# Low parts of weights from GpSimd to VectorE, and sums of squares by TensorE, in the first stage of a two-layer encoder trunk

## The chip, the cores and the metric

The kernel runs on one core of one Trainium2 chip. The metric is the device time of one execution in microseconds (us), taken as the median of several runs. A second, profiled execution leaves a trace of what each engine did: TensorE (PE, with its weight loads apart as PEld), VectorE (DVE), ScalarE (ACT), GpSimd (POOL) and SyncE (SP, which here issues every DMA).

## The reference

Two layers over x of 512 rows and 2048 columns, float32. Each layer is conditioned by a vector c of 2048: a product with a 2048 x 6144 matrix gives a shift, a scale and a gate.

```python
shift, scale, gate = split(silu(c) @ w_mod + b_mod, 3)
h = rms_norm(x, norm_g) * (1.0 + scale) + shift
out = mixer(h)                # projection in, attention and convolution, or spatial gating; projection out
x = x + gate * out
```

`rms_norm` divides a row by the root of the mean of its squares. After the two layers there is one more `rms_norm`.

## The kernel before

Everything lies transposed: a page is 128 of the 2048 features by the 512 rows. x has 16 pages (`x_t[0]` to `x_t[15]`), and so has h. Products on TensorE are made in three passes, to keep float32 precision: each operand is split into a high part (a rounded copy, fp32r) and a low part (the rest), and `mm3` (lines 371 to 376) adds high x high, high x low and low x high.

The change lies in the first stage, up to about 262 us, in which h is made and already used:

- **The norm.** ScalarE squares the 16 pages of x (L656). VectorE adds the 16 squares up into one page (L660, L661). Four small products with ones sum that page over the features (L207), VectorE scales and adds EPS (L210), GpSimd takes the power -1/2 (L211), VectorE multiplies the identity by it (L218), one product spreads it over all partitions (L224), ScalarE copies it to `R` (L225).
- **The conditioning.** `mod_tile(n, nt)` (L250 to L258) loads 128 columns of the conditioning matrix as two tiles of 128x1024 (`mraw`, five buffers) and multiplies each by silu(c), with the sum kept (L255). A page of h needs two such pairs, four products: the scale's pair, after which L262 makes the factor `gsc`, and the shift's pair, which gives `mod`.
- **A page of h**, `modulated(kt)`: VectorE x * gsc * R into `tmp` (L610), ScalarE the high part (L614, the page `hh`), VectorE the low part (L617, the page `lh`).
- **Weights.** `split_w` loads a tile `wraw` (three buffers), ScalarE casts it to the high part `whi` (L674), and **GpSimd** subtracts for the low part `wlo` (L675). There are 16 tiles of 128x768 (`in_ab_wp`, one per page) and 48 of 128x512 (`in_ab_wg`).
- **TensorE.** Per page, `mm3` for six gates: 18 matmuls of 512 columns, which need `hh`, `lh`, `whi` and `wlo`. For every four pages and each of three groups g, `quarter(g, q)` multiplies four pages with four tiles into two alternating PSUM banks: 48 matmuls, with a sum into SBUF after each 12 (ScalarE copies the first quarter, L699; VectorE adds the later ones, L701). Together 16 x 18 + 12 x 48 = 864 matmuls. The last of them, `quarter(2, 3)`, ends the stage; the projections and the attention follow on TensorE without a gap.

A scheduler fixes, when the program is built, the order in which each engine runs its instructions. At run time an engine takes them strictly in that order and waits at the first that isn't ready; SP's DMA issues are one such queue too.

```python
for kt in range(KT):
    with tc.issue_after(total.ins):
        mod_tile(pa, "ab", KT + kt, 5)
    mod_scale("ab", kt)
    mod_tile(pa, "ab", kt, 5)
    hi, lo = split_w(ab_wp[kt], W_P, work, 2)
    modulated("ab", kt, x_t[kt], r0, h.add())
```

`issue_after(total.ins)` puts the first products behind the last addition of squares (L661).

Of the kernel before, what the change touches and what calls it, by code (L numbers as in the profile page):

```python
# [9 lines left out]
F32 = mybir.dt.float32  # L10
F32R = mybir.dt.float32r
AF = mybir.ActivationFunctionType
ALU = mybir.AluOpType

D = 2048
S = 512
P = 128
KT = D // P
NT = S // P
HEADS = 8  # L20
GROUPS = 8
EPS = 1e-6
# [4 lines left out]
ALL, LEFT, RIGHT = slice(0, S), slice(0, S // 2), slice(S // 2, S)  # L27
# [88 lines left out]
def trunk(ctx, tc, xT, vecs, ab_wm, sg_wm, ab_wp, ab_wg, ab_wi, ab_wo, sg_wi, sg_wo, wsT, bs, rope, band, eye, out):  # L116
    nc = tc.nc
# [9 lines left out]
    def page(tag, bufs, dt=F32, pool=None):  # L127
        return (pool or work).tile([P, S], dt, tag=tag, bufs=bufs, name=tag)
# [44 lines left out]
    def bank():  # L173
        return psum.tile([P, S], F32, tag="ps", name="ps")
# [6 lines left out]
    ones = const.tile([P, P], F32, name="ones")  # L181
# [9 lines left out]
    x_t = Pages()  # L191
# [5 lines left out]
    def v1(c):  # L197
        return vec[:, c:c + 1]


    def inverse(parts, cols=ALL):
        n = (cols.stop - cols.start) // P
        sums = [bank() for _ in range(n)]
        for j, s in enumerate(parts):
            for i, acc in enumerate(sums):
                ts = slice(cols.start + i * P, cols.start + (i + 1) * P)
                nc.tensor.matmul(acc[:, 0:1], lhsT=s[:, ts], rhs=ones[:, 0:1], start=j == 0, stop=j == len(parts) - 1)  # L207
        r4 = const.tile([P, NT], F32, tag="r4", bufs=2, name="r4")
        for i, acc in enumerate(sums):
            nc.vector.tensor_scalar(out=r4[:, i:i + 1], in0=acc[:, 0:1], scalar1=1.0 / D, scalar2=EPS, op0=ALU.mult, op1=ALU.add)  # L210
        nc.gpsimd.tensor_tensor(out=r4[:, :n], in0=r4[:, :n], in1=mhalf[:, :n], op=ALU.pow)  # L211
        return r4

    def rms(parts, cols=ALL):
        r4, n = inverse(parts, cols), (cols.stop - cols.start) // P
        dg = page("tmp", 4)
        for i in range(n):
            nc.vector.tensor_scalar(out=dg[:, i * P:(i + 1) * P], in0=ident, scalar1=r4[:, i:i + 1], scalar2=None, op0=ALU.mult)  # L218
        return dg

    def spread(dg, r, cols=ALL):
        n = cols.stop - cols.start
        pr = bank()
        nc.tensor.matmul(pr[:, :n], lhsT=ones, rhs=dg[:, :n], start=True, stop=True)  # L224
        nc.scalar.copy(out=r[:, cols], in_=pr[:, :n])  # L225
# [24 lines left out]
    def mod_tile(pool, n, nt, bufs):  # L250
        src, b = wm[n]
        for h in range(2):
            raw = pool.tile([P, HALF], F32, tag="mraw", bufs=bufs, name="mraw")
            nc.sync.dma_start(out=raw, in_=src[nt, h])
            nc.vector.tensor_tensor_reduce(  # L255
                out=raw, in0=raw, in1=cb[:, h * HALF:(h + 1) * HALF], scale=0.5,
                scalar=v1(b + nt) if h == 0 else macc[n][:, nt:nt + 1], op0=ALU.mult, op1=ALU.add,
                accum_out=(mods if h else macc)[n][:, nt:nt + 1])  # L258

    def mod_scale(n, kt):  # L260
        g = v1((V_ABG if n == "ab" else V_SGG) + kt)
        nc.vector.scalar_tensor_tensor(  # L262
            out=gsc[n][:, kt:kt + 1], in0=mods[n][:, KT + kt:KT + kt + 1], scalar=1.0, in1=g,
            op0=ALU.add, op1=ALU.mult)
# [106 lines left out]
    def mm3(acc, w, m, first, last, **kw):  # L371


        nc.tensor.matmul(acc, lhsT=w[0], rhs=m[0], start=first, stop=False, **kw)  # L374
        nc.tensor.matmul(acc, lhsT=w[0], rhs=m[1], start=False, stop=False, **kw)  # L375
        nc.tensor.matmul(acc, lhsT=w[1], rhs=m[0], start=False, stop=last, **kw)  # L376

    class Pos:
# [3 lines left out]
        def slice(self):  # L382
            w = self.s.next(self.i, self.more)
            self.i += 1
            if self.tick:
                self.tick(self.s.last.ins)
            return w
# [216 lines left out]
                    mm3(acc, (a[0][:, ts], a[1][:, ts]), (hi[:, cs], lo[:, cs]), kt == 0, kt == KT - 1)  # L604
        return accs

    def modulated(n, kt, t, r, to, cols=ALL, keep=False):

        xr = page("tmp", 4)
        nc.vector.scalar_tensor_tensor(  # L610
            out=xr[:, cols], in0=t[:, cols], scalar=gsc[n][:, kt:kt + 1], in1=r[:, cols], op0=ALU.mult, op1=ALU.mult)
        hi, lo = to
        sh = mods[n][:, kt:kt + 1]
        nc.scalar.activation(out=hi[:, cols], in_=xr[:, cols], func=AF.Identity, bias=sh)  # L614
        if keep:
            nc.scalar.activation(out=t[:, cols], in_=xr[:, cols], func=AF.Identity, bias=sh)
        nc.vector.scalar_tensor_tensor(  # L617
            out=lo[:, cols], in0=xr[:, cols], scalar=sh, in1=hi[:, cols].bitcast(F32), op0=ALU.add, op1=ALU.subtract)

    def twice_silu(acc, s):  # L620

# [27 lines left out]
    h = Parts()  # L649
    pos = Pos(s_abi, s_abo)  # L650
    pa = tc.alloc_tile_pool(name="pa", bufs=2, reuse_waits="tile")
    parts = []
    squares = Book("hh", F32)
    for kt in range(KT):
        sq = squares.page()
        nc.scalar.activation(out=sq, in_=x_t[kt], func=AF.Square)  # L656
        if kt < 2:
            parts.append(sq)
        else:
            nc.vector.tensor_tensor(out=parts[kt % 2], in0=parts[kt % 2], in1=sq, op=ALU.add)  # L660
    total = nc.vector.tensor_tensor(out=parts[0], in0=parts[0], in1=parts[1], op=ALU.add)  # L661
    r0 = page("R", 2)
    spread(rms(parts[:1]), r0)

    def split_w(src, n, pool, bufs):
        raw = work.tile([P, HALF], F32, tag="wraw", bufs=3, name="wraw")[:, :n]
        size = HALF if pool is work else n  # L670
        hi = pool.tile([P, size], F32R, tag="whi", bufs=bufs, name="whi")[:, :n]
        lo = pool.tile([P, size], F32R, tag="wlo", bufs=bufs, name="wlo")[:, :n]
        nc.sync.dma_start(out=raw, in_=src)
        nc.scalar.copy(out=hi, in_=raw)  # L674
        nc.gpsimd.tensor_tensor(out=lo, in0=raw, in1=hi.bitcast(F32), op=ALU.subtract)  # L675
        return hi, lo

    gates = [bank() for _ in range(6)]
    sums, held = {}, {}

    def fetch(g, kts):
        for kt in kts:
            held[g, kt] = split_w(ab_wg[g, kt], S, pa, 8)

    def quarter(g, q):
        if q == 0:
            sums[g] = pa.tile([P, 4, S], F32, tag="sum", bufs=1, name="sum") if g == 1 else work.tile([P, 4, S], F32, tag="xy", bufs=4, name="xy")
        for f in range(4):
            acc = bank()
            cs = slice(f * P, (f + 1) * P)  # L690
            for i in range(4):
                kt = 4 * q + i
                (hi, lo), a = held[g, kt], h[kt]
                if g:
                    mm3(acc, (hi[:, cs], lo[:, cs]), a, i == 0, i == 3)
                else:
                    mm3(acc, (a[0][:, cs], a[1][:, cs]), (hi, lo), i == 0, i == 3)
            if q == 0:
                nc.scalar.copy(out=sums[g][:, f], in_=acc)  # L699
            else:  # L700
                nc.vector.tensor_tensor(out=sums[g][:, f], in0=acc, in1=sums[g][:, f], op=ALU.add)  # L701

    for kt in range(KT):
        with tc.issue_after(total.ins):
            mod_tile(pa, "ab", KT + kt, 5)
        mod_scale("ab", kt)
        mod_tile(pa, "ab", kt, 5)
        hi, lo = split_w(ab_wp[kt], W_P, work, 2)
        modulated("ab", kt, x_t[kt], r0, h.add())
        for f in range(6):  # L710
            cs = slice(f * P, (f + 1) * P)
            mm3(gates[f], (hi[:, cs], lo[:, cs]), h[kt], kt == 0, kt == KT - 1)
        fetch(0, [kt])
        q, i = divmod(kt, 4)
        if q:
            at = 4 * (q - 1) + 2 * (i % 2)
            fetch(1 + i // 2, [at, at + 1])
            if i % 2:
                quarter(1 + i // 2, q - 1)
        if i == 3:  # L720
            quarter(0, q)
# [188 lines left out]
    h = Parts()  # L910
# [22 lines left out]
    parts = right()  # L933
# [6 lines left out]
    for part in (0, 2):  # L940
        for kt in range(KT):
            hi, lo = ws[kt // 2]
# [56 lines left out]
    for n in range(4):  # L999
# [3 lines left out]
        for j in range(NT):  # L1003
            t = y.g[n][:, j]
# [3 lines left out]
    for i in range(2):  # L1008
        acc = bank()
# [61 lines left out]
    for g in range(2):  # L1071
        for i in range(2):
            turned_block(g, i)
    parts = right()
    r4 = inverse(parts, RIGHT)
    for f in (KT - 2, KT - 1):
        nc.scalar.activation(out=x3[f][:, RIGHT], in_=x3[f][:, RIGHT], func=AF.Copy, scale=v1(V_FG + f))
# [4 lines left out]
    for i in range(2):  # L1082
        for g in range(4):
            t = fin[i][:, g]
# [4 lines left out]
            if g % 2:  # L1089
                (nc.scalar if g > 1 else nc.sync).dma_start(  # L1090
                    out=out[1].rearrange("(t p n) -> t p n", t=2, p=P)[i, :, (g - 1) * S:(g + 1) * S].rearrange("p (g s) -> p g s", g=2),
                    in_=fin[i][:, g - 1:g + 1])
    left = out[0].rearrange("(f p n) -> f p n", f=KT, p=P)
    for f in range(KT):
        t = x3[f][:, LEFT]
# [81 lines left out]
```

## Time and profile before

| what | value |
|---|---|
| median of 3 runs | 1674.51 us (1673.35 to 1674.95) |
| profiled execution, its own time | 1674.59 us |
| span of its trace, first to last instruction | 1672.5 us |
| PE busy | 1616.3 us, 97% |
| DVE busy | 1307.8 us, 78% |
| ACT busy | 664.5 us, 40% |
| POOL busy | 146.0 us, 9% |

The profiled execution's own time is 2.1 us above its span. Busy shares are means over the whole span; the change is in the first sixth, and there the shares are others. A busy PE is not a PE at its peak, since the ends of matmuls are modelled: what counts is how many matmuls of 512 columns it starts in a stretch.

### The profile page before, as it was taken

To read this page: it belongs to the slowest core of one execution; us is meant where nothing else is said; L and a number is where in the kernel's file an instruction comes from. 1 tells how busy PE (TensorE), PEld (TensorE's weight loads), DVE (VectorE), ACT (ScalarE), POOL (GpSimd) and SP (SyncE) were. 2 spreads that over 40 slices of the span, in tenths; PEclk is the share of its full clock that TensorE was granted. 3 is DMA by queue.
4 is the path that set the end of the run, shared out by engine and by line. 5 is a ranking of instruction groups with operands and counts; after the bars stand their busy time and mean duration, and the time that the engine had idled before them with its cause. 6 is when DMAs were issued, how large, how long until landed. Compare 5 with 4: busy or idle time off the path is not lost.

```text
span 1672.5 us, 24676 instructions
## 1 busy us (share of the span) xinstructions
PE 1616.3 (97%) x9900; PEld 1442.9 (86%) x9900; DVE 1307.8 (78%) x1761; ACT 664.5 (40%) x953; POOL 146.0 (9%) x95
## 2 busy tenths in 40 slices
PE   4799899999999999999999999999999999999998
PEld 3677787888888888888889998999999999998998
DVE  7899738867765867677778878787988788898884
ACT  3232234323322323233544545444444444465552
POOL 2466531000000000000000000000000000000000
PEclk7999999999999999999999999999999999999999
DMA  8777534665666666655364351333233323335333
GB/s 314 255 266 271 199 111 160 223 219 196 218 214 232 233 211 215 213 199 195 102 217 138 124 170 57 107 110 102 87 114 95 118 94 119 96 100 200 105 98 115
DMA packets 85538, 276.44 MB, mean 165 GB/s; under 512 B 8752, under 2 KB 11056, under 8 KB 85424
## 3 DMA queue, kind: packets, MB, share of 16 engines
q1 hardware_dynamic: 85136, 273.82, 48.7%
q8 instruction: 77, 1.26, 0.3%
q10 hardware_dynamic: 288, 1.05, 0.2%
q14 instruction: 37, 0.30, 0.1%
HBM read 266.45 MB, written 8.39 MB: 164 GB/s over the span
## 4 chain that ended last, share of the span: by engine, by line
PE 82%; DVE 11%; issue 3%; ACT 2%; DMA 1%; SPq 0%; POOL 0%; POOLq 0%; DVEq 0%; ACTq 0%
PE ps L376 27%; PE ps L374 27%; PE ps L375 27%; DVE mraw L255 4%; DVE wlo L310 1%; PE ps L1028 1%; PE ps L783 1%; DVE gsc_ab L262 1%; ACT whi L309 1%; DMA xy<-in_xT_dram 1%; DVE lh L617 0%; ACT hh L614 0%; DVE st L1007 0%; DVE third L310 0%; DVE wraw L318 0%
## 5 line engine op out<-in xcount | busy, mean ns | idle before, releaser
L374 PE MATMUL ps<-hh,whi 128*128 128x512 f32 (+1 forms) x1600 | 570.1, 359 | 21.7 <-ACT hh L614 16.3
L375 PE MATMUL ps<-lh,whi 128*128 128x512 f32 (+1 forms) x1600 | 569.0, 356 | 1.5 <-DVE lh L845 1.5
L376 PE MATMUL ps<-hh,wlo 128*128 128x512 f32 (+1 forms) x1600 | 568.9, 356 | 1.2 <-DVE wlo L310 1.2
L374 PEld LDWEIGHTS ps<-hh,whi 128*128 128x128 f32 x1600 | 305.4, 191 | 68.9 <-ACT hh L614 20.0
L309 ACT CAST whi<-wraw 128x1024 fp32r<-128x1024 f32 x190 | 199.8, 1052 | 399.4 <-PE ps L375 289.9
L375 PEld LDWEIGHTS ps<-lh,whi 128*128 128x128 f32 x1600 | 305.0, 191 | 44.0 <-DVE lh L845 1.9
L376 PEld LDWEIGHTS ps<-hh,wlo 128*128 128x128 f32 x1600 | 304.9, 191 | 44.1 <-DVE wlo L310 1.7
L310 DVE TENSOR_TENSOR wlo<-wraw,whi 128x1024 fp32r<-128x1024 f32 x190 | 232.5, 1225 | 107.1 <-ACT whi L309 106.5
L255 DVE CUSTOM_DVE_ANT_0 mraw<-mraw,cb,vec 128x1024 f32<-128x1024 f32 x96 | 138.2, 1440 | 21.4 <-DMA mraw<-in_sg_wm_dram 16.7
L675 POOL TENSOR_TENSOR wlo<-wraw,whi 128x512 fp32r<-128x512 f32 (+1 forms) x64 | 117.2, 1851 | 104.6 <-ACT whi L674 97.9
L376 PE MATMUL ps<-sum,wlo 128*128 128x256 f32 x408 | 113.0, 277 | 0.9 <-DVE wlo L310 0.9
L374 PE MATMUL ps<-sum,whi 128*128 128x256 f32 x408 | 112.7, 276 | 0.0
L375 PE MATMUL ps<-sum,whi 128*128 128x256 f32 x408 | 112.7, 276 | 0.0
L374 PE MATMUL ps<-whi,hh 128*128 128x512 f32 (+1 forms) x288 | 102.8, 357 | 2.1 <-DVE xy L701 2.0
L309 ACT CAST whi<-first 128x1024 fp32r<-128x1024 f32 x56 | 58.8, 1050 | 114.0 <-DVE first L318 65.9
L375 PE MATMUL ps<-wlo,hh 128*128 128x512 f32 (+1 forms) x288 | 102.1, 354 | 0.3 <-POOL wlo L675 0.3
L376 PE MATMUL ps<-whi,lh 128*128 128x512 f32 (+1 forms) x288 | 102.1, 355 | 0.0
L310 DVE TENSOR_TENSOR wlo<-first,whi 128x1024 fp32r<-128x1024 f32 x56 | 68.3, 1220 | 24.8 <-ACT whi L309 24.8
L255 DVE CUSTOM_DVE_ANT_0 mraw<-mraw,cb,macc_ab 128x1024 f32<-128x1024 f32 x48 | 76.3, 1591 | 3.1 <-DMA mraw<-in_ab_wm_dram 2.1
L376 PEld LDWEIGHTS ps<-sum,wlo 128*128 128x128 f32 x408 | 76.6, 188 | 1.4 <-DVE wlo L310 1.4
L318 DVE TENSOR_TENSOR first<-first,wraw 128x1024 f32<-128x1024 f32 x63 | 76.7, 1217 | 0.5
L375 PEld LDWEIGHTS ps<-sum,whi 128*128 128x128 f32 x408 | 76.6, 188 | 0.0
(255 smaller groups left out, 2861.4 us busy)
## 6 DMA issues: line engine op xcount, KB each, us to landing
mraw<-in_ab_wm_dram SPq DMA_DIRECT2D x96, 512.0 KB, 4.6
mraw<-in_sg_wm_dram SPq DMA_DIRECT2D x96, 512.0 KB, 4.5
wraw<-in_ab_wi_dram SPq DMA_DIRECT2D x92, 512.0 KB, 3.7
wraw<-in_sg_wi_dram SPq DMA_DIRECT2D x75, 512.0 KB, 3.5
wraw<-in_ab_wo_dram SPq DMA_DIRECT2D x27, 512.0 KB, 3.5
wraw<-in_sg_wo_dram SPq DMA_DIRECT2D x27, 512.0 KB, 3.5
wraw<-in_ab_wg_dram SPq DMA_DIRECT2D x48, 256.0 KB, 2.9
first<-in_sg_wi_dram SPq DMA_DIRECT2D x21, 512.0 KB, 3.5
```

What stands on the lines that cost most here:

```text
L255: nc.vector.tensor_tensor_reduce(out=raw, in0=raw, in1=cb[:, h * HALF:(h + 1) * HALF], scale=0.5, scalar=v1(b + nt) if h == 0 else macc[n] ...
L262: nc.vector.scalar_tensor_tensor(out=gsc[n][:, kt:kt + 1], in0=mods[n][:, KT + kt:KT + kt + 1], scalar=1.0, in1=g, op0=ALU.add, op1=ALU.mult)
L309: nc.scalar.copy(out=hi, in_=raw)
L310: nc.vector.tensor_tensor(out=lo, in0=raw, in1=hi.bitcast(F32), op=ALU.subtract)
L318: nc.vector.tensor_tensor(out=r[a], in0=r[a], in1=r[b], op=ALU.add)
L374: nc.tensor.matmul(acc, lhsT=w[0], rhs=m[0], start=first, stop=False, **kw)
L375: nc.tensor.matmul(acc, lhsT=w[0], rhs=m[1], start=False, stop=False, **kw)
L376: nc.tensor.matmul(acc, lhsT=w[1], rhs=m[0], start=False, stop=last, **kw)
L675: nc.gpsimd.tensor_tensor(out=lo, in0=raw, in1=hi.bitcast(F32), op=ALU.subtract)
L783: nc.tensor.transpose(out=pt[:, i * P:(i + 1) * P], in_=ps[i][:, ks], identity=ident)
L1028: nc.tensor.matmul(accs[f][:, j * P:(j + 1) * P], lhsT=y.g[n][:, j, f * P:(f + 1) * P], rhs=wst[g // 4][:, g % 4 * P:(g % 4 + 1) * P], sta ...
```

## The change

Three edits, all in the first stage.

1. `split_w`: the subtraction that makes `wlo` is issued on VectorE, no longer on GpSimd.
2. The squares: no additions on VectorE. Each page of squares is the moving operand (512 columns) of a product whose weights are a single column of ones, so that the sums stand in one row of 512 in PSUM. ScalarE copies that row, four small products turn it into a column of four, and the rest of the norm is as before, with one instruction for L210 where there were four.
3. `modulated` takes `meanwhile`: the next page's scale pair (two products and `gsc`) is emitted inside it, and the low part of a page is placed behind the first of these two products. The first page's pair stands ahead of the loop, with no `issue_after`.

```diff
-        r4, n = inverse(parts, cols), (cols.stop - cols.start) // P
+        return diagonal(inverse(parts, cols), (cols.stop - cols.start) // P)
...
+        with ExitStack() as after:
+            if meanwhile:
+                after.enter_context(tc.issue_after(meanwhile()))
+            nc.vector.scalar_tensor_tensor(
+                out=lo[:, cols], in0=xr[:, cols], scalar=sh, in1=hi[:, cols].bitcast(F32), op0=ALU.add, op1=ALU.subtract)
...
+    row = bank()
     for kt in range(KT):
         sq = squares.page()
         nc.scalar.activation(out=sq, in_=x_t[kt], func=AF.Square)
-        if kt < 2:
-            parts.append(sq)
-        else:
-            nc.vector.tensor_tensor(out=parts[kt % 2], in0=parts[kt % 2], in1=sq, op=ALU.add)
-    total = nc.vector.tensor_tensor(out=parts[0], in0=parts[0], in1=parts[1], op=ALU.add)
+        nc.tensor.matmul(row[0:1], lhsT=ones[:, 0:1], rhs=sq, start=kt == 0, stop=kt == KT - 1)
+    line = page("tmp", 4)
+    nc.scalar.copy(out=line[0:1], in_=row[0:1])
+    turned = bank()
+    for i in range(NT):
+        nc.tensor.matmul(turned[:, i:i + 1], lhsT=line[0:1, i * P:(i + 1) * P], rhs=ones[0:1, 0:1], start=True, stop=True)
     r0 = page("R", 2)
-    spread(rms(parts[:1]), r0)
+    spread(diagonal(root([turned[:, :NT]], NT), NT), r0)
...
-        nc.gpsimd.tensor_tensor(out=lo, in0=raw, in1=hi.bitcast(F32), op=ALU.subtract)
+        nc.vector.tensor_tensor(out=lo, in0=raw, in1=hi.bitcast(F32), op=ALU.subtract)
...
+    def scale(kt):
+        began = mod_tile(pa, "ab", KT + kt, 5)
+        mod_scale("ab", kt)
+        return began
+
+    scale(0)
     for kt in range(KT):
-        with tc.issue_after(total.ins):
-            mod_tile(pa, "ab", KT + kt, 5)
-        mod_scale("ab", kt)
         mod_tile(pa, "ab", kt, 5)
         hi, lo = split_w(ab_wp[kt], W_P, work, 2)
-        modulated("ab", kt, x_t[kt], r0, h.add())
+        modulated("ab", kt, x_t[kt], r0, h.add(), meanwhile=(lambda: scale(kt + 1)) if kt < KT - 1 else None)
```

The lines move by 7 to 19 in the changed file: L255 is L262 there, L262 is L272, L610 is L621, L617 is L631, L675 is L691, L701 is L717.

The order that VectorE gets, between the copies of `cb` (silu(c) spread out) and the first page's L610. Each product is an `ISA` row on `mraw`, with a second row that reads its sum. Before:

```order
L661 TENSOR_TENSOR hh<-hh 128x512
L255 ISA mraw,macc_ab<-mraw,cb,vec 128x1024
L255 ISA macc_ab 128x1
L210 TENSOR_SCALAR r_172<-ps 128x1 x4
L255 ISA mraw,mod_ab<-mraw,cb,macc_ab 128x1024
L255 ISA mod_ab 128x1
L218 TENSOR_SCALAR tmp<-ident,r_172 128x128 x4
```

And from the same place of the changed program:

```order
L262 ISA mraw,mod_ab<-mraw,cb,macc_ab 128x1024
L262 ISA mod_ab 128x1
L691 TENSOR_TENSOR wlo<-wraw,whi 128x768
L215 TENSOR_SCALAR r_173<-ps 128x4
L262 ISA mraw,macc_ab<-mraw,cb,vec 128x1024
L262 ISA macc_ab 128x1
L225 TENSOR_SCALAR tmp<-ident,r_173 128x128 x4
L262 ISA mraw,mod_ab<-mraw,cb,macc_ab 128x1024
L262 ISA mod_ab 128x1
L691 TENSOR_TENSOR wlo<-wraw,whi 128x512
```

Four products stand ahead of L215 now (the last of them is the first row shown) and two more, with two low parts of weights, ahead of the first L621; before, four products stood ahead of the first L610.

VectorE again, one page further on in the loop, between the `tmp` of two pages. Before:

```order
L610 SCALAR_TENSOR_TENSOR tmp<-xy,gsc_ab,R 128x512
L255 ISA mraw,macc_ab<-mraw,cb,vec 128x1024
L255 ISA macc_ab 128x1
L255 ISA mraw,mod_ab<-mraw,cb,macc_ab 128x1024
L255 ISA mod_ab 128x1
L617 SCALAR_TENSOR_TENSOR lh<-tmp,mod_ab,hh 128x512
L255 ISA mraw,macc_ab<-mraw,cb,vec 128x1024
L255 ISA macc_ab 128x1
L255 ISA mraw,mod_ab<-mraw,cb,macc_ab 128x1024
L255 ISA mod_ab 128x1
L262 SCALAR_TENSOR_TENSOR gsc_ab<-mod_ab,vec 128x1
```

Now, from the `tmp` of page 4 to that of page 5:

```order
L621 SCALAR_TENSOR_TENSOR tmp<-xy,gsc_ab,R 128x512
L262 ISA mraw,macc_ab<-mraw,cb,vec 128x1024
L262 ISA macc_ab 128x1
L262 ISA mraw,mod_ab<-mraw,cb,macc_ab 128x1024
L262 ISA mod_ab 128x1
L691 TENSOR_TENSOR wlo<-wraw,whi 128x768
L262 ISA mraw,macc_ab<-mraw,cb,vec 128x1024
L262 ISA macc_ab 128x1
L631 SCALAR_TENSOR_TENSOR lh<-tmp,mod_ab,hh 128x512
L262 ISA mraw,mod_ab<-mraw,cb,macc_ab 128x1024
L262 ISA mod_ab 128x1
L691 TENSOR_TENSOR wlo<-wraw,whi 128x512
```

The low part of the page (L617, now L631) has moved behind one more product, and the low parts of the weights stand between the products.

TensorE at the start of the program. Before:

```order
L241 MATMUL ps<-ident,cs 128x128 x16
L207 MATMUL ps<-ones,hh 128x1 x4
L224 MATMUL ps<-tmp,ones 128x512
L374 MATMUL ps<-hh,whi 128x512 x6
```

And now:

```order
L248 MATMUL ps<-ident,cs 128x128 x16
L672 MATMUL ps<-hh,ones 1x512 x16
L677 MATMUL ps<-ones,tmp 128x1 x4
L231 MATMUL ps<-tmp,ones 128x512
L384 MATMUL ps<-hh,whi 128x512 x6
```

Sixteen products over 512 columns stand ahead of the small ones; nothing else in TensorE's first rows has moved.

## Rows read from the trace of the kernel before

**Rows 1.** The page, busy us, share of the span and instructions by engine.
```profile
PE 1616.3 (97%) x9900; PEld 1442.9 (86%) x9900; DVE 1307.8 (78%) x1761; ACT 664.5 (40%) x953; POOL 146.0 (9%) x95
```

**Rows 2.** Stretches: us, busy us of PE, PEld, DVE, ACT, POOL (instructions), clock, DMA.
```profile
12.00:14.00 2.00, 0.00 (x0) 0.00 (x0) 2.00 (x5) 1.87 (x5) 0.00 (x0) 0.98 1.07 417
14.00:16.00 2.00, 0.00 (x0) 0.00 (x0) 2.00 (x4) 1.50 (x3) 0.00 (x0) 0.50 1.03 421
...
100.00:120.00 20.00, 17.26 (x69) 13.74 (x69) 17.92 (x19) 8.36 (x14) 12.42 (x7) 0.91 0.79 271
```

**Rows 3.** Who waited for whom, 26 to 262 us: total us, times, longest.
```profile
POOL wlo L675 <- ACT whi L674: 97.9, 29, 13.0
...
PE ps L374 <- ACT hh L614: 16.3, 6, 3.0
...
PE ps L374 <- DVE xy L701: 4.8, 3, 2.8
...
PE ps L374 <- DVE sum L701: 2.0, 1, 2.0
```

**Rows 4.** VectorE by form, 20 to 262 us: busy us, mean ns, idle before.
```profile
L255 DVE CUSTOM_DVE_ANT_0 mraw<-mraw,cb,macc_ab 128x1024 f32<-128x1024 f32 x32 | 55.9, 1747 | 0.8
L255 DVE CUSTOM_DVE_ANT_0 mraw<-mraw,cb,vec 128x1024 f32<-128x1024 f32 x31 | 51.5, 1661 | 1.4 <-DMA mraw<-in_ab_wm_dram 1.4
L617 DVE SCALAR_TENSOR_TENSOR lh<-tmp,mod_ab,hh 128x512 fp32r<-128x512 f32 x16 | 19.2, 1201 | 10.4 <-ACT hh L614 10.4
...
L610 DVE SCALAR_TENSOR_TENSOR tmp<-xy,gsc_ab,R 128x512 f32<-128x512 f32 x16 | 15.0, 937 | 0.8 <-ACT R L225 0.2
L262 DVE SCALAR_TENSOR_TENSOR gsc_ab<-mod_ab,vec 128x1 f32<-128x1 f32 x16 | 14.8, 922 | 0.4
```

**Rows 5.** Timeline, VectorE then GpSimd, around 60 us: start us, us, instruction.
```profile
52.72 1.67 DVE L262 SCALAR_TENSOR_TENSOR gsc_ab<-mod_ab,vec 128x1 f32<-128x1 f32 x1
54.52 0.75 DVE L610 SCALAR_TENSOR_TENSOR tmp<-xy,gsc_ab,R 128x512 f32<-128x512 f32 x1
55.19 1.28 DVE L255 CUSTOM_DVE_ANT_0 mraw<-mraw,cb,vec 128x1024 f32<-128x1024 f32 x1
...
56.51 1.28 DVE L255 CUSTOM_DVE_ANT_0 mraw<-mraw,cb,macc_ab 128x1024 f32<-128x1024 f32 x1
...
62.92 0.16 DVE L262 SCALAR_TENSOR_TENSOR gsc_ab<-mod_ab,vec 128x1 f32<-128x1 f32 x1
...
51.78 2.60 POOL L675 TENSOR_TENSOR wlo<-wraw,whi 128x768 fp32r<-128x768 f32 x1 [1.51 <-ACT whi L674]
```

**Rows 6.** Timeline, the high part of page 3 and the stage's last two sums.
```profile
57.83 0.72 ACT L614 ACTIVATE hh<-tmp,mod_ab 128x512 fp32r<-128x512 f32 x1 [6.13 <-DVE mod_ab L255]
...
258.82 0.69 DVE L701 TENSOR_TENSOR xy<-ps,xy 128x512 f32<-128x512 f32 x1 [2.03 <-PE ps L376]
261.54 0.69 DVE L701 TENSOR_TENSOR xy<-ps,xy 128x512 f32<-128x512 f32 x1 [2.03 <-PE ps L376]
```

**Rows 7.** Timeline of the norm: start us, us, instruction.
```profile
3.73 5.42 PE L241 MATMUL ps<-ident,cs 128*128 128x128 f32 x32 [3.73 <-DMA ident<-in_eye_dram]
...
11.45 6.10 DVE L660 TENSOR_TENSOR hh<-hh 128x512 f32<-128x512 f32 x10
...
18.33 1.87 PE L207 MATMUL ps<-ones,hh 128*128 128x1 f32 x8 [9.19 <-DVE hh L661]
...
23.57 2.05 PE L224 MATMUL ps<-tmp,ones 128*128 128x512 f32 x2 [3.37 <-DVE gsc_ab L262]
25.65 0.58 ACT L225 COPY R<-ps 128x512 f32<-128x512 f32 x1 [10.05 <-PE ps L224]
...
26.27 0.75 DVE L610 SCALAR_TENSOR_TENSOR tmp<-xy,gsc_ab,R 128x512 f32<-128x512 f32 x1 [0.25 <-ACT R L225]
```

**Rows 8.** Groups by form, 300 us on: TensorE, then VectorE; busy us, mean ns.
```profile
L1010 PE MATMUL ps<-R,ones 128*128 128x512 f32 x4 | 1.9, 592 | 0.0
...
L310 DVE TENSOR_TENSOR wlo<-wraw,whi 128x1024 fp32r<-128x1024 f32 x115 | 140.4, 1222 | 87.4 <-ACT whi L309 87.0
```

More of the change, by code (lines that the diff above doesn't have):

```diff
@@ L207, in inverse, with root @@
                 nc.tensor.matmul(acc[:, 0:1], lhsT=s[:, ts], rhs=ones[:, 0:1], start=j == 0, stop=j == len(parts) - 1)
+        return root([acc[:, 0:1] for acc in sums], n)
+    def root(sums, n):
         r4 = const.tile([P, NT], F32, tag="r4", bufs=2, name="r4")
+        w = n // len(sums)
         for i, acc in enumerate(sums):
-            nc.vector.tensor_scalar(out=r4[:, i:i + 1], in0=acc[:, 0:1], scalar1=1.0 / D, scalar2=EPS, op0=ALU.mult, op1=ALU.add)
+            nc.vector.tensor_scalar(out=r4[:, i * w:(i + 1) * w], in0=acc, scalar1=1.0 / D, scalar2=EPS, op0=ALU.mult, op1=ALU.add)
         nc.gpsimd.tensor_tensor(out=r4[:, :n], in0=r4[:, :n], in1=mhalf[:, :n], op=ALU.pow)
@@ L214, in rms, with diagonal @@
     def rms(parts, cols=ALL):
-        r4, n = inverse(parts, cols), (cols.stop - cols.start) // P
+        return diagonal(inverse(parts, cols), (cols.stop - cols.start) // P)
+    def diagonal(r4, n):
         dg = page("tmp", 4)
@@ L254, in mod_tile @@
             nc.sync.dma_start(out=raw, in_=src[nt, h])
-            nc.vector.tensor_tensor_reduce(
+            product = nc.vector.tensor_tensor_reduce(
                 out=raw, in0=raw, in1=cb[:, h * HALF:(h + 1) * HALF], scale=0.5,
@@ L258, in mod_tile @@
                 accum_out=(mods if h else macc)[n][:, nt:nt + 1])
+            if not h:
+                began = product.ins
+        return began
     def mod_scale(n, kt):
@@ L605, in tmajor, with modulated @@
         return accs
-    def modulated(n, kt, t, r, to, cols=ALL, keep=False):
+    def modulated(n, kt, t, r, to, cols=ALL, keep=False, meanwhile=None):
         xr = page("tmp", 4)
@@ L616, in modulated @@
             nc.scalar.activation(out=t[:, cols], in_=xr[:, cols], func=AF.Identity, bias=sh)
-        nc.vector.scalar_tensor_tensor(
-            out=lo[:, cols], in0=xr[:, cols], scalar=sh, in1=hi[:, cols].bitcast(F32), op0=ALU.add, op1=ALU.subtract)
+        with ExitStack() as after:
[3 more added lines that the diff above has]
+                out=lo[:, cols], in0=xr[:, cols], scalar=sh, in1=hi[:, cols].bitcast(F32), op0=ALU.add, op1=ALU.subtract)
     def twice_silu(acc, s):
@@ L651, in trunk @@
     pa = tc.alloc_tile_pool(name="pa", bufs=2, reuse_waits="tile")
-    parts = []
     squares = Book("hh", F32)
+    row = bank()
     for kt in range(KT):
@@ L701, in quarter @@
                 nc.vector.tensor_tensor(out=sums[g][:, f], in0=acc, in1=sums[g][:, f], op=ALU.add)
+    def scale(kt):
+        began = mod_tile(pa, "ab", KT + kt, 5)
+        mod_scale("ab", kt)
+        return began
+    scale(0)
     for kt in range(KT):
-        with tc.issue_after(total.ins):
-            mod_tile(pa, "ab", KT + kt, 5)
-        mod_scale("ab", kt)
         mod_tile(pa, "ab", kt, 5)
         hi, lo = split_w(ab_wp[kt], W_P, work, 2)
-        modulated("ab", kt, x_t[kt], r0, h.add())
+        modulated("ab", kt, x_t[kt], r0, h.add(), meanwhile=(lambda: scale(kt + 1)) if kt < KT - 1 else None)
         for f in range(6):
```

## Prediction

> **What bounds the kernel now.** I read the page first: TensorE is busy 97% of the span [rows 1], so time can only be won where it starts fewer matmuls than it could. The change touches the first stage alone, so I read that one by stretches: from 100 to 120 us TensorE is busy 17.26 us at a granted clock of 0.91 and starts 69 matmuls [rows 2]. At full rate the last two sums of the stage stand 2.72 us apart, with 12 matmuls between them [rows 6]: 0.2267 us each, 88 in 20 us. In the same stretch VectorE is busy 17.92 us [rows 2]. The waits say what TensorE lacked: 16.3 us for `hh`, the page whose `tmp` and `mod` VectorE makes, and 4.8 and 2.0 us for a PSUM bank that VectorE's sums empty late [rows 3]. So VectorE limits the stage, through its order.
>
> Why is VectorE so busy? By form, its means are far above single instructions: products 1747 and 1661 ns, the low part of a page 1201, `tmp` 937, `gsc` 922 [rows 4]. The timeline shows a product in 1.28 us, a `tmp` in 0.75, a `gsc` of one column in 0.16 and in 1.67 [rows 5]. The long `gsc` runs from 52.72 to 54.39, and a subtraction of GpSimd from 51.78 to 54.38 [rows 5]: the one ends with the other. Against the short durations (0.75 for the low part too) the excess is 32 x 0.467 + 31 x 0.381 + 16 x 0.451 + 16 x 0.187 + 16 x 0.762 = 49 us.
>
> The Trainium skill (SBUF — State Buffer, Who interferes with whom) says that a VectorE instruction with two SBUF inputs and a GpSimd instruction that reads SBUF exclude each other, and that the loser blocks for the whole instruction. The trace agrees in kind with the 1.67 us. If each of the 64 subtractions cost VectorE half of a length like 2.60 us, the rule would make it 83 us, not 49; the end would not move by that, as TensorE takes over as the bound in either case.
>
> **Part 1, subtractions on VectorE.** The 64 low parts cost there: a 128x1024 takes 1.22 us [rows 8], ten 128x512 additions follow each other in 6.10, 0.61 each [rows 7]; back to back a 1024 should take twice the columns at about 1.14, and a 128x768 lies between, 0.88 (my estimate). 16 x 0.88 + 48 x 0.61 = 43 us added, 49 us taken away. By totals alone that is 6 us and proves little; the order decides.
>
> Per page VectorE has four products at 1.32 us (start to start, [rows 5]), `gsc` 0.16, `tmp` and low part at 0.67 (start to start, [rows 5]), one 768 and three 512: 5.28 + 0.16 + 1.34 + 0.88 + 1.83 = 9.5 us, and with three sums per page in the later pages 11.3. TensorE needs 18 + 36 = 54 matmuls per page from page 4 on, 12.2 us. So TensorE becomes the bound there, if VectorE doesn't wait for more than 1 to 2.7 us per page.
>
> **Part 2, the squares.** The 15 additions leave VectorE before 18.3 us [rows 7]. That is worth nothing by itself, since all waits for `R`; and `R` comes later now. The products with `ident` end at 3.73 + 5.42 = 9.15 [rows 7]; then 16 products of 512 columns in float32 follow. The nearest row is L1010 at full clock: two such products, four records of 592 ns, busy 1.9 us [rows 8], so records start 0.44 apart and a product takes 0.87. They end at 9.15 + 13.9 = 23.1. A copy as long as L225's, 0.58 [rows 7], gives 23.7, four small products 1.87 at most [rows 7], 25.6. From there to the first `tmp` before: 18.33 + 1.87 = 20.20 to 26.27, 6.07 us [rows 7], of which the spreading product took 2.05 at half clock; at full clock it would save 1.0. So `tmp` of page 0 starts between 30.6 and 31.7; I take 31.2, 4.9 later than before.
>
> VectorE's queue stands behind L215 meanwhile: two products and two low parts are behind it, and SP's loads behind their buffers. They fit in the gap up to 31.2.
>
> **Part 3, the order.** By 31.2 VectorE has done six products and two weights' low parts, where it had four products. From the first `tmp` to the high part of page 3 the new order has 10 products, 7 `tmp` and low parts, two 768, two 512 and three `gsc`: 13.2 + 4.7 + 1.8 + 1.2 + 0.5 = 21.4, so page 3 is ready to be cast at 52.6. Before, it was at 57.83 [rows 6]. **First term: 5.2 us.** The wait for ScalarE's `hh` in front of the low part, 10.4 us in sum [rows 4], is covered now: 1.32 of a product behind `tmp`, against some 0.8 needed.
>
> From page 3 to the last sum at 261.54 [rows 6] TensorE starts 864 - 54 = 810 matmuls, 183.6 us, and 0.7 for the cast: 184.4, where it took 203.7. So 19.3 us were lost there. What stays lost? After the short first pages TensorE will have sat idle again and begin page 3 at half clock: the clock of 0.91 over 20 us [rows 2] prices such a fall at 1.8. And in pages 12 to 15, where ScalarE's casts wait for tiles that TensorE still uses, low parts and sums come late in VectorE's order: I take 4 of the 4.8 + 2.0 us of bank waits [rows 3]. So 6 of 19.3 stay, **second term: 13.3 us**. Bounds: nothing stays lost (19.3), or all of it (0).
>
> All behind the stage is unchanged and moves with it. Sum: 18.5 us off the profiled execution's 1674.6, 1656.1. The median, 1674.51, is the same within 0.1. Bounds of this sum: 1650 with no loss left, 1669.4 with all of it.
>
> **Rivals.**
>
> *The row of ones runs at half clock (0.13).* The granted clock was 0.98 from 12 to 14 us and 0.50 from 14 on [rows 2], with TensorE idle since 9.15. If one column of weights does not hold it up, 5.6 products are done by 14 and 10.4 take 1.74 each, to 32.1: 9 us later, 1665; with 2.05 each [rows 7], 1668. Against it: TensorE never pauses there now. The Trainium skill (TensorE: Matmul & The Clock Gate, Part 1) says that the throttled state is the default and activity releases it. By that all 16 would start slow, 1670. The trace does not agree for this start: the clock was 0.98 with TensorE idle [rows 2].
>
> *The losses only change their cause (0.12).* TensorE still starts 69 where 88 fit, now waiting for sums behind low parts. Then only the first term is left: 1669.
>
> *VectorE inherits GpSimd's waits, slower (0.07).* GpSimd waited 97.9 us for ScalarE's casts [rows 3], 1.53 per tile, and harmed nobody. VectorE in that place holds products, pages and sums behind it. Behind page 15 at least 18 + 144 matmuls remain, 36.7 us; the end stays where it was if page 15 is cast at 224.8, that is, at 14.35 us per page from 52.6. Against a load of 10.5 (20 sums over 12 pages) that is 3.9 us of waits per page, 0.96 per tile: from there on it is slower. With the full 1.53 per tile a page takes 16.6, page 15 is cast at 252, and the time is 1701; at 1.1 per tile, about 1681. Against it: those were waits of an engine with nothing else to do, while VectorE reaches each low part only after products; the loads that must come, 271 GB/s in the stretch shown, are well under the 417 of the start [rows 2].
>
> *No change (0.06).* 5 us won at page 3 and lost again to bank waits: 1671 to 1678.
>
> **How the numbers follow.** My forecast has 0.62, with a range of its own of 1650 to 1664. 0.2% is 3.3 us, about what a measurement here can tell from no change. Faster: 0.62 + 0.13 + 0.12, less a little where the rivals reach the bound, 0.86; same 0.07; slower 0.07. The range leaves out the slower cases, no change, and a tip of either end: 1649 to 1670.
>
> **What would show it.** No VectorE product above 1.3 us and no `gsc` above 0.2 up to 260 us; the 16 row products at 0.87 us with a clock of 1.0; first `tmp` near 31; page 3 cast near 53; 53 to 54 matmuls per 12.2 us from there; the last sum near 243. I am wrong if VectorE waits for ScalarE's casts by about 4 us per page, or if the clock falls before 23 us.

## The result, and the profile after

The changed kernel takes 1647.61 us in the median of 4 runs (1646.27 to 1648.98), beside 1673.93 us for the kernel before (4 runs): ratio 0.9844, 95% interval 0.9832 to 0.9855. That is 26 us faster. The forecast was 1656 with 1649 to 1670: it had the direction, missed the size by 8 us, and the time lies just below its range.

The profiled execution took 1647.22 us with a span of 1645.1. Its busy shares, from the page:

```profile
PE 1617.7 (98%) x9932; PEld 1438.3 (87%) x9932; DVE 1289.8 (78%) x1807; ACT 665.7 (40%) x954; POOL 29.4 (2%) x31
```

TensorE is as busy in microseconds as before [rows 1]; GpSimd lost 117 us of work, and VectorE, which took all of it over, is busy 18 us *less*. Some 10 of these are the additions of squares that part 2 took away; with part 1 alone VectorE is busy 1299.7 us, still 8 less than before. The forms show how. VectorE by form, 20 to 245 us of the changed kernel (busy us, mean ns, idle before):

```profile
L262 DVE CUSTOM_DVE_ANT_0 mraw<-mraw,cb,vec 128x1024 f32<-128x1024 f32 x32 | 41.0, 1280 | 1.4 <-DMA mraw<-in_ab_wm_dram 1.4
L262 DVE CUSTOM_DVE_ANT_0 mraw<-mraw,cb,macc_ab 128x1024 f32<-128x1024 f32 x31 | 39.7, 1280 | 0.2
L691 DVE TENSOR_TENSOR wlo<-wraw,whi 128x512 fp32r<-128x512 f32 x48 | 32.4, 689 | 9.2 <-ACT whi L690 8.8 <-PE ps L385 0.4
...
L691 DVE TENSOR_TENSOR wlo<-wraw,whi 128x768 fp32r<-128x768 f32 x16 | 15.3, 955 | 3.3 <-ACT whi L690 3.3
L621 DVE SCALAR_TENSOR_TENSOR tmp<-xy,gsc_ab,R 128x512 f32<-128x512 f32 x16 | 12.0, 748 | 1.1 <-ACT R L232 1.0
L631 DVE SCALAR_TENSOR_TENSOR lh<-tmp,mod_ab,hh 128x512 fp32r<-128x512 f32 x16 | 12.0, 748 | 0.8 <-ACT hh L625 0.8
...
L272 DVE SCALAR_TENSOR_TENSOR gsc_ab<-mod_ab,vec 128x1 f32<-128x1 f32 x15 | 2.3, 153 | 0.0
```

Beside [rows 4]: products 1280 ns where they were 1747 and 1661, `gsc` 153 where it was 922, the low part of a page 748 where it was 1201. The wait in front of that low part is 0.8 us in sum, from 10.4. In exchange VectorE waits 12 us for ScalarE's casts (8.8 + 3.3), 0.19 per tile.

Five moments of the stage, from the timeline (start us, us, instruction): the row of ones, the spreading product, the first `tmp`, the high part of page 3, and the stage's last sum:

```profile
8.81 13.89 PE L672 MATMUL ps<-hh,ones 128*1 128x512 f32 x32
...
27.64 2.07 PE L231 MATMUL ps<-tmp,ones 128*128 128x512 f32 x2 [3.23 <-DVE tmp L225]
...
30.37 0.75 DVE L621 SCALAR_TENSOR_TENSOR tmp<-xy,gsc_ab,R 128x512 f32<-128x512 f32 x1 [0.97 <-ACT R L232]
...
50.35 0.72 ACT L625 ACTIVATE hh<-tmp,mod_ab 128x512 fp32r<-128x512 f32 x1 [2.87 <-DVE mod_ab L262]
...
234.67 0.69 DVE L717 TENSOR_TENSOR xy<-ps,xy 128x512 f32<-128x512 f32 x1 [2.03 <-PE ps L386]
```

Beside [rows 6, 7]: the first `tmp` is 4.1 us later than before, page 3 is 7.5 us earlier, the last sum 26.9 us earlier. From the last sum to the end of the span it was 1411.0 us before and is 1410.4 now: nothing behind the stage changed.

TensorE in stretches of the changed kernel (us, busy us and instructions, granted clock, DMA share, GB/s):

```profile
36.00:46.00 10.00, 10.00 (x42) 0.91 0.89 308
46.00:56.00 10.00, 9.68 (x43) 1.00 0.97 340
...
106.00:116.00 10.00, 10.00 (x46) 1.00 0.84 309
```

46 instructions in 10 us is the full rate with those that reach over an edge; before, the stretch from 100 to 120 us had 69 in 20 us, at a clock of 0.91 [rows 2].

### The profile page after: what moved, and what is told of

Read it like the earlier page. It is cut to its first block, busy times and chain, and to the rows that moved or that the text cites. A ratio compares the mean times of both kernels' runs of the same rounds, so it can differ in the third digit from the quotient of the medians.

```text
span 1645.1 us, 24676 instructions
## 1 busy us (share of the span) xinstructions
PE 1617.7 (98%) x9932; PEld 1438.3 (87%) x9932; DVE 1289.8 (78%) x1807; ACT 665.7 (40%) x954; POOL 29.4 (2%) x31
## 4 chain that ended last, share of the span: by engine, by line
PE 85%; DVE 9%; issue 2%; DMA 2%; ACT 2%; POOL 0%; SPq 0%; DVEq 0%; POOLq 0%; ACTq 0%
PE ps L386 27%; PE ps L385 27%; PE ps L384 27%; DVE mraw L262 2%; DVE wlo L320 1%; DMA mraw<-in_ab_wm_dram 1%; PE ps L1047 1%; PE ps L672 1%; PE ps L802 1%; DVE wlo L691 1%; DMA wraw<-in_ab_wg_dram 1%; ACT whi L319 1%; DVE st L1026 0%; DVE third L320 0%; DVE wraw L328 0%
## 5 line engine op out<-in xcount | busy, mean ns | idle before, releaser
L384 PE MATMUL ps<-hh,whi 128*128 128x512 f32 (+1 forms) x1600 | 563.7, 355 | 2.7 <-ACT hh L625 2.2
L262 DVE CUSTOM_DVE_ANT_0 mraw<-mraw,cb,vec 128x1024 f32<-128x1024 f32 x96 | 127.0, 1323 | 25.5 <-DMA mraw<-in_sg_wm_dram 14.3
L384 PEld LDWEIGHTS ps<-sum,whi 128*128 128x128 f32 x408 | 76.6, 188 | 0.0
L385 PEld LDWEIGHTS ps<-sum,whi 128*128 128x128 f32 x408 | 76.6, 188 | 0.0
L690 ACT CAST whi<-wraw 128x512 fp32r<-128x512 f32 (+1 forms) x64 | 42.4, 674 | 80.3 <-DMA wraw<-in_ab_wp_dram 28.1
```

Of the source, the lines that this page charges most:

```text
L262: product = nc.vector.tensor_tensor_reduce(out=raw, in0=raw, in1=cb[:, h * HALF:(h + 1) * HALF], scale=0.5, scalar=v1(b + nt) if h == 0 el ...
```

## The experiments

Two theories of where VectorE's time came from. **A, collisions:** GpSimd's subtractions stop VectorE's two-input instructions while they run; moving them ends that. **B, order and dependence:** the gain is in the covered waits, the freed start and in no longer depending on GpSimd's queue; the place of the subtraction is worth little (43 us added for 49 taken away).

Four kernels undo or isolate one part each.

**Part 1 undone.**

```diff
-        nc.vector.tensor_tensor(out=lo, in0=raw, in1=hi.bitcast(F32), op=ALU.subtract)
+        nc.gpsimd.tensor_tensor(out=lo, in0=raw, in1=hi.bitcast(F32), op=ALU.subtract)
```

> The changed kernel with the low parts of weights back on GpSimd; the squares by products with ones and the order by meanwhile stay. Theory A, collisions: what VectorE won is GpSimd's subtractions no longer stopping its two-input instructions. Then products average about 1.7 us again, gsc about 0.9, and the second term (19 us between page 3 and the last sum) is lost; part 3 still covers waits for the cast, so the ratio to before is 0.993 to 1.000. Theory B, order: 43 us added against 49 taken away means that the place of the subtraction hardly matters, and the gain is parts 2 and 3; then the ratio stays at 0.986 to 0.989.

Measured: 1669.18 us, ratio 0.9974 (0.9964 to 0.9985). Parts 2 and 3 without part 1 win 0.3%. VectorE is stretched again:

```profile
L262 DVE CUSTOM_DVE_ANT_0 mraw<-mraw,cb,macc_ab 128x1024 f32<-128x1024 f32 x31 | 51.8, 1672 | 0.7 <-DMA mraw<-in_ab_wm_dram 0.4
...
L631 DVE SCALAR_TENSOR_TENSOR lh<-tmp,mod_ab,hh 128x512 fp32r<-128x512 f32 x16 | 20.0, 1251 | 6.1 <-ACT hh L625 6.1
...
L272 DVE SCALAR_TENSOR_TENSOR gsc_ab<-mod_ab,vec 128x1 f32<-128x1 f32 x15 | 11.6, 772 | 0.4
```

**Part 1 alone**, the same line edited the other way in the kernel before.

```diff
-        nc.gpsimd.tensor_tensor(out=lo, in0=raw, in1=hi.bitcast(F32), op=ALU.subtract)
+        nc.vector.tensor_tensor(out=lo, in0=raw, in1=hi.bitcast(F32), op=ALU.subtract)
```

> The kernel before with part 1 alone: the 64 subtractions on VectorE, squares and order as before. Theory A: most of the 19 us of the second term is won, and the start is not delayed by 4 us; ratio 0.984 to 0.990. Theory B: by totals 6 us less on VectorE, but the low parts of pages wait for the cast with nothing in front of them, 10 us in sum as before; ratio 0.994 to 1.000.

Measured: 1648.58 us, ratio 0.9854 (0.9838 to 0.9871). One word of the diff brings all but what the intervals can't tell. Part 3's covered waits were not needed for that: with the subtractions on VectorE the scheduler finds something to put in front of the low part, and it waits 0.0 us here:

```profile
L617 DVE SCALAR_TENSOR_TENSOR lh<-tmp,mod_ab,hh 128x512 fp32r<-128x512 f32 x16 | 11.9, 747 | 0.0
```

**Part 2 undone.**

```diff
-        nc.tensor.matmul(row[0:1], lhsT=ones[:, 0:1], rhs=sq, start=kt == 0, stop=kt == KT - 1)
+        if kt < 2:
+            parts.append(sq)
+        else:
+            nc.vector.tensor_tensor(out=parts[kt % 2], in0=parts[kt % 2], in1=sq, op=ALU.add)
...
+    spread(rms(parts[:1]), r0)
```

> The changed kernel with part 2 undone: the squares added on VectorE again, four small products, four instructions for L215. R should be ready near 26 instead of 30.3 us, with two products fewer done by then. If the late R costs what it is late, this is 3 to 4 us faster than the changed kernel, ratio 0.982 to 0.983. If the work that VectorE does in that gap makes up for it, and the stage is set by VectorE's total up to page 3, the ratio is 0.984 to 0.987.

Measured: 1647.14 us, ratio 0.9841 (0.9826 to 0.9856), the changed kernel's within the intervals. The first `tmp` starts 2.9 us earlier than in the changed kernel, and page 3 is cast 0.6 us later:

```profile
27.50 0.75 DVE L621 SCALAR_TENSOR_TENSOR tmp<-xy,gsc_ab,R 128x512 f32<-128x512 f32 x1 [0.78 <-ACT R L232]
...
50.99 0.72 ACT L625 ACTIVATE hh<-tmp,mod_ab 128x512 fp32r<-128x512 f32 x1 [1.72 <-DVE mod_ab L262]
```

**Part 3 undone.**

```diff
-    scale(0)
     for kt in range(KT):
+        scale(kt)
         mod_tile(pa, "ab", kt, 5)
...
-        modulated("ab", kt, x_t[kt], r0, h.add(), meanwhile=(lambda: scale(kt + 1)) if kt < KT - 1 else None)
+        modulated("ab", kt, x_t[kt], r0, h.add())
```

> The changed kernel with part 3 undone: the scale pair stands ahead of each page again, and the page's low part follows tmp as the scheduler likes. If the covered wait for the cast (0.7 us a page, 10 us in all before) is on the path, page 3 is cast 2 to 3 us later and the ratio is 0.986 to 0.988. If TensorE sets the pace from page 4 on and only three pages count, it is within 0.001 of the changed kernel's 0.9844.

Measured: 1647.45 us, ratio 0.9843 (0.9828 to 0.9858): worth nothing, with part 1 in place.

So it is part 1. But this does not yet tell a collision from a dependence: on GpSimd the low parts also come through another queue. The next two kernels give GpSimd work that nobody waits for.

**GpSimd beside it, reading.** `scrap` is a page that no one reads.

```diff
         nc.vector.tensor_tensor(out=lo, in0=raw, in1=hi.bitcast(F32), op=ALU.subtract)
+        nc.gpsimd.tensor_tensor(out=scrap[:, :n], in0=hi.bitcast(F32), in1=hi.bitcast(F32), op=ALU.subtract)
```

> The changed kernel, plus 64 subtractions on GpSimd of the same shapes, right after each cast, which read whi twice and write a scrap page that nobody reads. Nothing waits for them, so they can act on VectorE only by being at work beside it. Theory A, collisions: VectorE's two-input instructions (products, tmp, low parts, gsc, and now the 64 subtractions too) are stretched again, by 49 us or more in sum; VectorE then needs over 12.6 us a page, TensorE waits, and the ratio to before is 0.995 to 1.015, slower than the changed kernel by 18 us or more. Theory B, it was the dependence (TensorE and VectorE waiting for GpSimd's results and queue): nothing changes, 0.984 to 0.986.

Measured: 1690.8 us, ratio 1.0096 (1.0071 to 1.0121): 43 us slower than the changed kernel, and slower than the kernel before. VectorE first, then GpSimd's own:

```profile
L262 DVE CUSTOM_DVE_ANT_0 mraw<-mraw,cb,macc_ab 128x1024 f32<-128x1024 f32 x31 | 46.1, 1487 | 0.2
L693 DVE TENSOR_TENSOR wlo<-wraw,whi 128x512 fp32r<-128x512 f32 x42 | 46.0, 1110 | 1.5 <-PE ps L385 1.0 <-ACT whi L692 0.5
L262 DVE CUSTOM_DVE_ANT_0 mraw<-mraw,cb,vec 128x1024 f32<-128x1024 f32 x31 | 44.4, 1432 | 0.0
L693 DVE TENSOR_TENSOR wlo<-wraw,whi 128x768 fp32r<-128x768 f32 x16 | 20.1, 1256 | 4.9 <-ACT whi L692 4.9
L631 DVE SCALAR_TENSOR_TENSOR lh<-tmp,mod_ab,hh 128x512 fp32r<-128x512 f32 x16 | 17.3, 1082 | 0.8 <-ACT hh L625 0.8
...
L694 POOL TENSOR_TENSOR scrap<-whi 128x512 f32<-128x512 f32 x48 | 70.2, 1462 | 80.9 <-ACT whi L692 78.7
```

The excess over the changed kernel's means is 31 x 0.207 + 31 x 0.152 + 42 x 0.421 + 16 x 0.301 + 16 x 0.334 = 39 us in these rows; with `tmp`, `gsc` and the 512s after 245 us it is 46, a little under the 49 expected. TensorE's waits (time, count, longest, 30 to 250 us) are back:

```profile
PE ps L384 <- ACT hh L625: 8.7, 5, 2.5
PE ps L385 <- DVE lh L631: 6.8, 6, 2.4
PE ps L384 <- DVE xy L720: 6.4, 3, 2.8
PE ps L384 <- DVE sum L720: 6.0, 2, 3.2
```

No result of GpSimd is used. All that it could hold up is the next cast into a `whi` that it still reads, and no wait of ScalarE's in this trace is put down to GpSimd. So theory B's dependence can't do this: collision it is. The trace of the kernel before shows the same within one run, by start and end times: of the 32 products in the first of [rows 4], the 12 with no subtraction of GpSimd beside them took 1281 ns on average, the 20 others 2026.

**GpSimd beside it, writing.**

```diff
         nc.vector.tensor_tensor(out=lo, in0=raw, in1=hi.bitcast(F32), op=ALU.subtract)
+        nc.gpsimd.tensor_copy(out=scrap[:, 0:1], in_=hi[:, 0:1].bitcast(F32))
+        nc.gpsimd.memset(scrap[:, :n], 0.0)
```

> As the last one, but GpSimd reads one column only and then fills a page of the same width with zeros, so that it writes as much and reads next to nothing. If it is GpSimd's reading that excludes VectorE's second input, products stay at 1.28 us and gsc at 0.15, ratio 0.984 to 0.986. If any work of GpSimd on the memory does it, the stretching is that of the run before, ratio over 0.993.

Measured: 1650.63 us, ratio 0.9869 (0.9845 to 0.9892); just above the 0.984 to 0.986 expected, but the interval overlaps the changed kernel's. VectorE runs at its short durations beside GpSimd's work, 61 us in the two groups shown last (by start and end times, VectorE's two-input instructions lie beside 30 of the 37 us of all memsets):

```profile
L262 DVE CUSTOM_DVE_ANT_0 mraw<-mraw,cb,macc_ab 128x1024 f32<-128x1024 f32 x31 | 39.8, 1283 | 0.8 <-DMA mraw<-in_ab_wm_dram 0.4
...
L693 DVE TENSOR_TENSOR wlo<-wraw,whi 128x512 fp32r<-128x512 f32 x48 | 32.4, 690 | 7.2 <-ACT whi L692 6.7 <-PE ps L385 0.4
...
L272 DVE SCALAR_TENSOR_TENSOR gsc_ab<-mod_ab,vec 128x1 f32<-128x1 f32 x15 | 2.3, 155 | 0.1
...
L694 POOL COPY scrap<-whi 128x1 f32<-128x1 f32 x64 | 36.1, 564 | 137.2 <-ACT whi L692 135.5
L695 POOL MEMSET scrap<- 128x512 f32 x48 | 25.3, 527 | 2.9
```

So it is GpSimd's reading of whole pages that stops VectorE. The Trainium skill (SBUF — State Buffer, Who interferes with whom) says just that: a VectorE instruction with two SBUF inputs contends with a GpSimd instruction that reads SBUF, not with one that only writes it. These two runs agree, with 1487 and 1283 ns for the same product.

**A shorter row.** The late `R` was the one cost that the change had. Here the squares are rounded to fp32r, without low parts, so that a row product is one pass:

```diff
-    squares = Book("hh", F32)
+    squares = Book("hh")
+    one = const.tile([P, 1], F32R, name="one")
+    nc.vector.tensor_copy(out=one, in_=ones[:, 0:1])
...
-        nc.tensor.matmul(row[0:1], lhsT=ones[:, 0:1], rhs=sq, start=kt == 0, stop=kt == KT - 1)
+        nc.tensor.matmul(row[0:1], lhsT=one, rhs=sq, start=kt == 0, stop=kt == KT - 1)
```

> The changed kernel with the squares written as fp32r and the column of ones too, so that a row product is one pass: the squares lose their low parts, the rest is as before. 16 products take 0.23 us each instead of 0.87 and are paced by the squares, which end near 15.7; R near 24 instead of 30.3. If the late R is on the path, the stage ends up to 5 us earlier, ratio 0.981 to 0.983. If loads set the pace by then (420 GB/s up to 28 us) or TensorE's clock takes it back, it is 0.984 to 0.985. Below 0.984 it beats both kernels.

Measured: 1649.97 us, ratio 0.9854 (0.9832 to 0.9876): no gain. `R` came 5 us earlier, and page 3 at the same time as in the changed kernel (50.35):

```profile
25.54 0.75 DVE L621 SCALAR_TENSOR_TENSOR tmp<-xy,gsc_ab,R 128x512 f32<-128x512 f32 x1
...
50.14 0.72 ACT L625 ACTIVATE hh<-tmp,mod_ab 128x512 fp32r<-128x512 f32 x1 [1.87 <-DVE mod_ab L262]
```

Over five kernels without collisions the first `tmp` starts anywhere from 25.5 to 30.9 us (part 1 alone 27.8, part 3 undone 30.9), page 3 is cast between 50.1 and 51.3, and the last sum starts between 234.0 and 236.1. The run with GpSimd's writes has 34.6, 51.4 and 236.2. So within this range `R` is not on the path. In all five VectorE does 16 products and 7 low parts of weights before page 3 is cast; from its first product on it is busy 30.2 to 31.1 us, and once the first `tmp` has begun it stands idle for 0.2 us at most. It is the same sum in any order, and a late `R` only means that products and weights' low parts come before it.

## Why the prediction was wrong in size

The direction and the mechanism were right: the excess of 49 us was GpSimd's, VectorE's load per page fell below TensorE's, and TensorE became the bound of the stage. By the prediction's own steps:

- **Part 1.** Forecast per tile 0.88 and 0.61 us start to start; the changed kernel shows durations of 955 and 689 ns, about 0.08 more, as start to start goes. Products, `tmp` and `gsc` fell to the short durations. The rival that VectorE inherits GpSimd's waits exists, at 0.19 us per tile where 0.96 would have been the turning point.
- **Part 2.** The row took 13.89 us (13.9 forecast), at full clock as assumed, and ended at 22.70 (23.1). The first `tmp` came at 30.37, forecast 31.2. (Of the two low parts said to stand behind L215, one stands ahead of it.) The rival of the half clock fell. Its remark that the trace does not agree with a throttled start misreads the clock column. In both kernels the first products with `ident` start 0.21 us apart and those after 7.1 us only 0.11, so TensorE did begin at half clock; the column reads 1.00 there because these traces have no record of the clock before 7 us. The row started at 8.81, after the clock had risen. That the lateness of `R` matters was assumed and is wrong: the runs with part 2 undone and with the shorter row moved `R` by 3 and 5 us and the time by nothing the intervals can tell. The second is the cleaner, since with part 2 undone the first product starts 1.7 us later too.
- **First term, 5.2 us forecast, 7.5 measured.** Page 3 was cast at 50.35, not 52.6: 0.8 us from `R`, and 1.4 from the sum behind it, 1.1 of it because I spaced all ten products at 1.32 us. That is the distance between two products; to any other instruction it is 1.2 (49.03 to 50.23 in the changed kernel).
- **Second term, 13.3 us forecast, 19.4 measured. This is the step that failed:** "6 of 19.3 stay". From the cast of page 3 to the last sum it is 184.3 us now, just the 184.4 that I had called the limit. Two things are in that. My count of 864 - 54 = 810 was too high: the scheduler puts 18 matmuls of `quarter(0, 0)` between the gates of the first three pages, in both kernels, so 792 remained. The limit was 4.1 us lower, the loss before 23.4 us, and what stays of it 4.0. And those 4.0 are less than my 6: the clock did not fall at page 3, since TensorE no longer idled there, and bank waits of VectorE's sums nearly vanished.

What I had not worked out is what the loss before was made of. Behind page 3's first gate TensorE waited 12.0 us: 5.2 for `hh`, 6.8 for banks. Its clock fell to half (1.2 GHz) at page 3 and behind the four longest of these waits, so that five stretches of 10 us have a mean of 0.83 and lose 1.7 us each, 8.5 in all. That leaves 2.9 of the 23.4 without a name. Two of the five, from the kernel before (us, busy us and instructions, clock, DMA share, GB/s):

```profile
76.00:86.00 10.00, 7.49 (x27) 0.83 0.90 306
106.00:116.00 10.00, 10.00 (x38) 0.83 0.77 260
```

I had counted one such fall. In the changed kernel the clock is 1.00 in every stretch from 46 us to that sum: the falls went with the waits.

The changed kernel's TensorE waits, 150 to 240 us, and the rows before page 3's gates begin at 51.13 (`whi,hh` is a quarter, `hh,whi` the gates):

```profile
PE ps L384 <- DVE xy L717: 0.4, 1, 0.4
```

```profile
50.18 0.39 PE L386 MATMUL ps<-whi,lh 128*128 128x512 f32 x1
50.41 0.39 PE L384 MATMUL ps<-whi,hh 128*128 128x512 f32 x1
50.63 0.39 PE L385 MATMUL ps<-wlo,hh 128*128 128x512 f32 x1
50.86 0.39 PE L386 MATMUL ps<-whi,lh 128*128 128x512 f32 x1
51.13 1.66 PE L384 MATMUL ps<-hh,whi 128*128 128x512 f32 x6
```

Together 2.3 + 4.1 + 2.0 = 8.4 us: but for rounding, the distance between the forecast of 243 for the last sum and 234.7. I had priced the remaining bank waits by those of before (4 of 6.8), though they were a product of the same late VectorE that the change cured; with VectorE ahead of TensorE they go with the rest. And the 1650 that I called the bound with no loss left was none: with 792 matmuls it is 1674.6 - 5.2 - 23.4 = 1646.0, below my whole range.

What is not settled: of the 4.0 us that remain between page 3 and the last sum, 1.7 are waits (1.3 for `lh`, 0.4 for a bank), and the rest was not followed one by one; and the runs do not tell whether parts 2 and 3 are worth a tenth of a per cent; the intervals are about as wide.

## What to carry to other kernels

Where VectorE's means by form lie far above its single instructions, look for GpSimd in the timeline before counting instructions: work handed to GpSimd that reads whole pages can cost VectorE as much as doing it itself (49 us against 48 here, with GpSimd's 117 on top). When a change lifts the engine that limits a stage above the next one, price the stage by the next one's full rate, and count its work from the order, not from the loop; waits caused by the old limit go with it. And a late result cost nothing here, for the 5 us tried, since the engine that waits for it still had other work of the same stage to do.

## What the runs showed that I had not expected

- GpSimd's extra reads hurt more (43 us) than the subtractions that were its own job (22 us, from part 1 undone). VectorE has 64 two-input instructions more to be stopped there, the low parts of weights at 1110 and 1256 ns; whether that is all of the difference was not tried.
- TensorE's clock did not fall through 13.9 us of products with one column of weights without a pause: 1.00 in each stretch. With the shorter row, where the products wait for the squares, it fell while they ran. The same 4 us, first of the changed kernel, then of the shorter row (columns as in [rows 2]):

```profile
16.00:20.00 4.00, 4.00 (x11) 0.79 (x10) 3.83 (x7) 0.00 (x0) 0.00 (x0) 1.00 1.03 419
```

```profile
16.00:20.00 4.00, 2.95 (x10) 1.92 (x10) 1.46 (x3) 1.02 (x2) 0.04 (x1) 0.50 1.02 406
```

In the changed kernel the clock fell later, in the pause before the gates. Between 28 and 32 us it is 0.50 there and 0.52 with the shorter row: the early `R` met a TensorE at half clock, and so did the late one.
